# Even attention: the keys' low part written once, and the heads' norms with joined diagonals, joined epsilons and a root of eight operations

## Chip, cores and metric

The kernel runs on one core of one Trainium2 chip. The metric is the device time of one execution in microseconds (us), lower is better. The time given for a kernel is the median of its runs. One execution was also recorded by the hardware profiler, and all rows of the profile are of that one. Engines carry the profile's names: PE is TensorE's matmuls and PEld its weight loads, DVE is VectorE, ACT is ScalarE, POOL is GpSimd, SP is SyncE (here it issues DMAs).

## What is computed

The reference is a small transformer of two layers in float32: 512 tokens (`x`) and 256 context tokens (`ctx`) of width 1024, each layer with a mixer and a gated feed-forward network, every part with a modulated norm in front. The change touches the mixer of layer 0, the even one. Beside a gated chunk network it holds a differential attention with four heads: each head has two components of 64 channels, two softmaxes over the 768 keys, and takes their difference.

```python
def diff_attn(q, k, v, lam):
    b, tq = q.shape[0], q.shape[1]
    tk = k.shape[1]
    s = jnp.einsum('bqhd,bkhd->bhqk', q, k).astype(jnp.float32) * ATTN_SCALE
    p = jax.nn.softmax(s, axis=-1).reshape(b, B_HEADS, 2, tq, tk)
    a = p[:, :, 0] - lam * p[:, :, 1]
    return jnp.einsum('bhqk,bkhe->bqhe', a.astype(v.dtype), v)

def diff_out(o, g, lam_init):
    b, t = o.shape[0], o.shape[1]
    return (rmsnorm(o, g) * (1.0 - lam_init)).reshape(b, t, B_V_WIDTH)
```

The 512 token queries see all 768 keys, the 256 context queries only the 256 context keys. `rmsnorm` divides by the root of the mean square plus 1e-6.

## The kernel before

**Layout.** Activations lie with channels on the 128 partitions and tokens along the free axis, 768 of them (512 tokens, then 256 context). A head's two components of 64 channels share one tile: component 0 on partitions 0 to 63, component 1 on 64 to 127.

**Products in two parts.** To keep float32 accuracy with the faster `float32r` matmuls, an operand is split into a rounded high part (a cast on ACT) and the remainder (a subtraction on DVE or POOL). A full product is three matmuls (`mm3`, L110 to 116): high by high, high by low, low by high.

**Scores.** For scores the split uses the spare rows of the 64-channel contraction. `stack_q` (L267) makes one 128-row tile per component: the query's high part on that component's own 64 partitions, its low part on the other 64. `stack_k` (L280) makes two tiles per component: `kh` with the key's high part on both halves, `kl` with the key's low part on both halves. Two accumulating passes over 128 rows, Q by `kh` and Q by `kl`, then give all four products. `kh` takes two ACT casts of 64x768 (L286, L287), `kl` two DVE subtractions of 64x768 (L289). All four key tiles of a head come from one tag of six buffers, the query tiles from a tag of three.

**A head.** `head` (L621) runs three query pairs. `attend` (L566) calls `softmax_diff` (L541) for two blocks of 128 queries: per component the two passes (L550 to 553; 512 token keys by L552, only for the first four blocks, and 256 context keys by L553), the row maximum on DVE (L554), the exponential on ACT with its row sum (L556), then on DVE the difference of the components (L560 to 562) and an epsilon for the later norm (L563: the square of the first component's sum times 1e-6, since the probabilities are left undivided). PE transposes the result (L574), ACT and DVE split it (L130, L131), and PE multiplies it with the split values (L114 to 116); ACT copies the head's output out (L586).

**Norm of a head.** It follows one head later, in steps: squares on ACT (L611), then `rstd_diag` (L153): matmuls with a tile of ones sum the squares over channels (L164), DVE adds the epsilons (L175), takes the inverse root by three Newton steps from an integer estimate (`rsqrt_small`, L139 to 148, ten instructions), and writes six 128x128 diagonals, one per block of tokens (L184); two matmuls of ones by the diagonals spread the factors over all partitions (L194), and DVE applies them (L619).

**Order of the work.** The code gives each instruction a priority, in the order in which it is written, but for blocks that are raised or held back explicitly. A planner then simulates the engines with durations of its own and gives each engine's queue, step by step, the instruction that can run, the more urgent first; a tile can be written as soon as a buffer of its tag is free. On the chip each queue runs strictly in the order found. Within `head`, the stacking of the next head is written behind the second query pair. To fill PE beside the attention there are the projections of the gated network (`gated`, L588; its weights are cast by ACT at L88 and L91's subtraction is done by POOL), gelu on ACT (L642), and transposes with statistics on DVE (`turn`, L648). All of this runs roughly from 150 to 330 us of the span. The odd attention of layer 1 (L1584 to L1633) is not touched.

Of the kernel before, what the change touches and what calls it, by code (L numbers as in the profile page):

```python
# [6 lines left out]
F32 = mybir.dt.float32  # L7
F32R = mybir.dt.float32r
BF16 = mybir.dt.bfloat16
I32 = mybir.dt.int32  # L10
AF = mybir.ActivationFunctionType
ALU = mybir.AluOpType
AX = mybir.AxisListType.X

P = 128
D = 1024
KT = D // P
TX = 512
TC = 256
TA = TX + TC  # L20
HID = 2816
NF = HID // P
EPS = 1e-6
ROOT = 0.703952253
# [3 lines left out]
class Builder:  # L28
# [251 lines left out]
    def stack_k(self, k, pool, T, tag, bufs):  # L280
        nc = self.nc
        out = []
        for X, Y in ((slice(0, 64), slice(64, 128)), (slice(64, 128), slice(0, 64))):
            kh = pool.tile([P, T], F32R, name=self.uid("kh"), tag=tag, bufs=bufs)
            kl = pool.tile([P, T], F32R, name=self.uid("kl"), tag=tag, bufs=bufs)
            nc.scalar.copy(kh[X], k[X])  # L286
            nc.scalar.copy(kh[Y], k[X])  # L287
            for Z in (X, Y):
                nc.vector.tensor_tensor(kl[Z], k[X], kh[X].bitcast(F32), ALU.subtract)  # L289
            out.append((kh, kl))  # L290
        return out


# [38 lines left out]
    def even(self):  # L332
        tc, nc, a = self.tc, self.nc, self.a
# [7 lines left out]
        def f3(tag="f3", bufs=8):  # L341
            return R1.tile([P, TA], F32, name=self.uid(tag), tag=tag, bufs=bufs)
# [4 lines left out]
        for k in range(0, KT, 2):  # L347
            t = self.load(Rh, a["xT"][k * P:(k + 2) * P, :].rearrange("(k p) t -> p k t", p=P), [P, 2, TX], f"hx{k}")
# [47 lines left out]
        sq = self.squares(hx, TX)  # L396
# [24 lines left out]
        qk = {}  # L421
# [37 lines left out]
        for half, heads in enumerate(((0, 1), (2, 3))):  # L459
# [3 lines left out]
            for k in range(KT):  # L463
                t = self.adap.tile([P, 2, 512], F32R, name=self.uid("wq"), tag="wq", bufs=3) if k % 3 == 2 else None
# [8 lines left out]
                if half == 0:  # L473
                    t, sh = hx[k], self.modcol(0, 0, k, 0)
# [35 lines left out]
        for k in range(KT):  # L510
            W = self.unit(a["v0"][k * P:(k + 1) * P, :], 512)
            for tb in range(6):
                c = slice(tb * P, (tb + 1) * P)
# [24 lines left out]
        Ra = tc.alloc_tile_pool(name="att0", bufs=1, side="right", reuse_waits="tile")  # L538
        oraw, raw = [], {}

        def softmax_diff(Q, K, qb, eps):  # L541


            koff = 0 if qb < 4 else TX
            qs = slice(qb * P, (qb + 1) * P)
            nm, sums = self.small(2, "sa", 10), self.small(2, "sa", 10)
            es = []
            for c in range(2):
                ps = self.wide()
                for p in range(2):  # L550
                    if qb < 4:
                        nc.tensor.matmul(ps[:, :TX], Q[c][:, qs], K[c][p][:, :TX], start=p == 0, stop=p == 1)  # L552
                    nc.tensor.matmul(ps[:, TX:TA], Q[c][:, qs], K[c][p][:, TX:], start=p == 0, stop=p == 1)  # L553
                nc.vector.tensor_reduce(nm[:, c:c + 1], ps[:, koff:TA], axis=AX, op=ALU.max, negate=True)  # L554
                e = Ra.tile([P, TA], F32, name=self.uid("e"), tag="e", bufs=6)
                self.last_exp = nc.scalar.activation(e[:, koff:], ps[:, koff:TA], AF.Exp, bias=nm[:, c:c + 1],  # L556
                                                     accum_out=sums[:, c:c + 1])
                es.append(e[:, koff:])
            r = self.small(1, "sa", 10)
            nc.vector.reciprocal(r, sums[:, 1:2])  # L560
            nc.vector.scalar_tensor_tensor(r, r, self.nlam, sums[:, 0:1], ALU.mult, ALU.mult)
            nc.vector.scalar_tensor_tensor(es[0], es[1], r, es[0], ALU.mult, ALU.add)
            nc.vector.scalar_tensor_tensor(eps[:, qb:qb + 1], sums[:, 0:1], EPS, sums[:, 0:1], ALU.mult, ALU.mult)  # L563
            return es[0]

        def attend(t, Q, K, qp, o, eps):  # L566
            es = [softmax_diff(Q, K, 2 * qp + i, eps) for i in range(2)]
            kbs = list(range(6)) if qp < 2 else [4, 5]
            po = self.bank()[:, :TC]
            for i in range(0, len(kbs), 2):  # L570
                pt = self.bank()
                for j in range(2):
                    for b in range(2):
                        nc.tensor.transpose(pt[:, j * TC + b * P:j * TC + (b + 1) * P],  # L574
                                            es[b][:, (i + j) * P:(i + j + 1) * P], self.ident)
                th = Ra.tile([P, 512], F32R, name=self.uid("ath"), tag="at", bufs=6)
                tl = Ra.tile([P, 512], F32R, name=self.uid("atl"), tag="at", bufs=6)
                self.split(th, tl, pt)
                for j in range(2):
                    kb = kbs[i + j]  # L580
                    c = slice(t * P, (t + 1) * P)
                    m = slice(j * TC, (j + 1) * TC)
                    self.mm3(po, (vhi[kb][:, c], vlo[kb][:, c]), (th[:, m], tl[:, m]),
                             i + j == 0, i + j == len(kbs) - 1)
            s = slice(qp * TC, (qp + 1) * TC)
            nc.scalar.copy(o[:, s], po)  # L586
# [10 lines left out]

        def stack(t):
            return (self.stack_q(qk[t], Ra, TA, "sq", 3, eng=nc.gpsimd if t == 3 else nc.vector),
                    self.stack_k(qk[4 + t], Ra, TA, "sk", 6))  # L600

        norms = {}

        def norm(t, step):

            if t not in norms:
                return
            o, eps = norms[t][:2]
            if step == 0:
                sq = self.sumsq()  # L610
                nc.scalar.activation(sq, o, AF.Square)  # L611
                norms[t] = o, eps, sq
            elif step == 1:
                sq = norms[t][2]
                norms[t] = o, eps, self.rstd_diag([(sq[:, :TX], TX), (sq[:, TX:], TC)], 1.0 / P, eps=eps)
            else:
                for off, T, dg in ((0, TX, norms[t][2][0]), (TX, TC, norms[t][2][1])):
                    c = o[:, off:off + T]
                    nc.vector.scalar_tensor_tensor(c, c, self.subg, self.spread(dg), ALU.mult, ALU.mult)  # L619

        def head(t):  # L621
            Q, K = QK.pop(t)
            o = f3("o", 4)
            eps = self.small(6, "sx", 2)
            for qp in range(3):
                attend(t, Q, K, qp, o, eps)
                if qp == 0:
                    norm(t - 1, 1)
                elif qp == 1:
                    if t < 3:  # L630
                        QK[t + 1] = stack(t + 1)
                    norm(t - 1, 2)
            norms[t] = o, eps
            norm(t, 0)
            if t == 3:
                norm(t, 1)
                norm(t, 2)
            oraw.append(o)
# [38 lines left out]
        with tc.high_priority(offset=tc.cur_priority - here):  # L677
            QK = {0: stack(0)}
        for t in range(2):
            head(t)  # L680
# [5 lines left out]
        with tc.high_priority(offset=tc.cur_priority - here), tc.issue_after(last.ins):  # L686
            head(2)
            head(3)
# [48 lines left out]
        sq, rest = self.sumsq(), []  # L737
# [1072 lines left out]
```

## Time and profile before

| | |
|---|---|
| median of 3 runs | 1576.95 us (1575.58 to 1578.64) |
| profiled execution | 1580.41 us |
| its span, first to last instruction | 1578.6 us |
| mean granted clock of TensorE | 0.990 |
| instructions | 24990 |
| DMA | 162.27 MB, mean 103 GB/s |

The profile's page gives busy times as shares of the span; a busy PE is not PE at its peak, since matmuls are pipelined and their shown durations overlap. Therefore the distance from one start to the next is the measure of what a matmul costs in a full queue. Rows of the timeline give the start, the duration, the engine, the line, the operation, output and inputs, and behind them in brackets the idle time of the engine just before and the instruction that ended it. Rows of a line's view give the count and the shortest, median and longest duration in ns. `L49` stands for lines of helpers that many parts share.

### The profile page before, as it was taken

The numbers are of one execution on the slowest core, as the hardware profiler recorded it, in microseconds if no ns is written. First come the engines' busy times: TensorE is split into PE (matmuls) and PEld (weight loads), VectorE is DVE, ScalarE is ACT, GpSimd is POOL, SyncE is SP. The second block draws the span as 40 slices with busy tenths as digits, with TensorE's granted clock in tenths as the row PEclk, the third lists the DMA queues.
The fourth block names the chain that finished last, engine by engine and source line by source line (L and its number), as shares of the span: only waits on it lengthen the run. The fifth ranks groups of instructions, "written<-read, shape, count | busy, mean of one in ns | idle before, by whom it ended". The sixth has DMA issues, their size and how long they took to land.

```text
span 1578.6 us, 24990 instructions
## 1 busy us (share of the span) xinstructions
PE 1517.3 (96%) x9563; PEld 1356.5 (86%) x9563; DVE 1078.7 (68%) x1938; ACT 727.8 (46%) x1490; POOL 826.8 (52%) x558
## 2 busy tenths in 40 slices
PE   6999988999999999999999999899999999999998
PEld 4776877889989999999999988677869889999997
DVE  4620788775697787888886486765667876666665
ACT  2422677553552333333333354555645644444444
POOL 0464211050347767767776544531314299898882
PEclk9999998999999999999999999999999999999999
DMA  8735100043123333345542211200225133333201
GB/s 330 310 129 202 44 8 1 1 134 134 67 74 114 113 102 127 127 146 168 162 158 88 79 47 36 66 28 15 68 87 207 48 105 105 105 99 109 93 21 54
DMA packets 53416, 162.27 MB, mean 103 GB/s; under 512 B 6192, under 2 KB 8624, under 8 KB 45616
## 3 DMA queue, kind: packets, MB, share of 16 engines
q1 hardware_dynamic: 46240, 135.37, 25.6%
q10 hardware_dynamic: 7056, 25.30, 4.9%
q8 instruction: 75, 1.23, 0.3%
q14 instruction: 45, 0.37, 0.1%
HBM read 158.55 MB, written 2.10 MB: 102 GB/s over the span
## 4 chain that ended last, share of the span: by engine, by line
PE 85%; DVE 10%; ACT 3%; issue 1%; DMA 0%; POOL 0%; DVEq 0%; SPq 0%; ACTq 0%; POOLq 0%
PE pw L114 12%; PE pw L115 12%; PE pw L116 11%; PE pb L115 8%; PE pb L116 8%; PE pb L114 8%; PE pf L114 4%; PE pf L115 4%; PE pf L116 4%; PE pb L1633 2%; PE pb L1622 2%; PE pf L369 2%; PE pw L1584 1%; PE pw L1592 1%; DVE t L49 1%
## 5 line engine op out<-in xcount | busy, mean ns | idle before, releaser
L115 PE MATMUL pw<-ax,w 128*128 128x384 f32 (+2 forms) x740 | 236.6, 320 | 4.2 <-DVE ax L49 2.2
L114 PE MATMUL pw<-ax,w 128*128 128x384 f32 (+2 forms) x740 | 235.8, 322 | 3.6 <-DVE q L49 1.9
L116 PE MATMUL pw<-ax,w 128*128 128x384 f32 (+2 forms) x740 | 236.1, 320 | 0.1
L784 DVE SCALAR_TENSOR_TENSOR xT<-pb,mod,xT 128x512 f32<-128x512 f32 (+3 forms) x204 | 143.2, 708 | 127.7 <-PE pb L116 127.3
L91 POOL TENSOR_TENSOR w<-raw,w 128x512 fp32r<-128x512 f32 (+1 forms) x76 | 114.9, 1521 | 218.2 <-ACT w L88 195.6
L49 POOL TENSOR_TENSOR w<-raw,w 128x512 fp32r<-128x512 f32 x122 | 185.9, 1539 | 48.5 <-ACT w L49 48.3
L49 POOL TENSOR_TENSOR w<-t,w 128x512 fp32r<-128x512 f32 x99 | 148.7, 1505 | 55.6 <-ACT w L49 55.6
L114 PE MATMUL pb<-hh,w 128*128 128x512 f32 x480 | 170.9, 356 | 2.3 <-DVE xT L784 2.3
L116 PE MATMUL pb<-hh,w 128*128 128x512 f32 x480 | 171.4, 357 | 0.0
L115 PE MATMUL pb<-hh,w 128*128 128x512 f32 x480 | 171.1, 356 | 0.0
L115 PE MATMUL pw<-T,w 128*128 128x384 f32 (+1 forms) x508 | 158.3, 312 | 2.3 <-DVE T L131 2.3
L114 PE MATMUL pw<-T,w 128*128 128x384 f32 (+1 forms) x508 | 157.8, 312 | 2.0 <-ACT T L130 1.5
L116 PE MATMUL pw<-T,w 128*128 128x384 f32 (+1 forms) x508 | 158.2, 312 | 0.0
L115 PEld LDWEIGHTS pw<-ax,w 128*128 128x128 f32 x740 | 140.7, 190 | 10.6 <-DVE ax L49 2.7
L114 PEld LDWEIGHTS pw<-ax,w 128*128 128x128 f32 x740 | 139.8, 190 | 10.8 <-DVE q L49 2.7
L114 PE MATMUL pf<-ax,w 128*128 128x256 f32 (+2 forms) x428 | 141.5, 331 | 4.2 <-ACT f L595 2.8
L116 PEld LDWEIGHTS pw<-ax,w 128*128 128x128 f32 x740 | 140.4, 190 | 3.5 <-DVE w L953 0.4
L115 PE MATMUL pf<-ax,w 128*128 128x256 f32 (+2 forms) x428 | 140.3, 328 | 0.0
L116 PE MATMUL pf<-ax,w 128*128 128x256 f32 (+2 forms) x428 | 140.1, 327 | 0.0
L49 POOL TENSOR_TENSOR hh<-hs,hh 128x768 fp32r<-128x768 f32 (+1 forms) x42 | 78.3, 1866 | 95.0 <-ACT hh L49 93.5
L49 POOL TENSOR_TENSOR w<-rawo,w 128x512 fp32r<-128x512 f32 x59 | 103.6, 1757 | 29.8 <-ACT w L49 29.8
L239 DVE SCALAR_TENSOR_TENSOR junk<-ar,cb 128x1024 bf16<-128x1024 f32 x64 | 105.7, 1651 | 0.0
(410 smaller groups left out, 3920.5 us busy)
## 6 DMA issues: line engine op xcount, KB each, us to landing
raw<-ffn_in SPq DMA_DIRECT2D x44, 1024.0 KB, 5.4
ar<-ada SPq DMA_DIRECT2D x24, 1024.0 KB, 7.4
ar<-ada ACTq DMA_DIRECT2D x48, 512.0 KB, 3.6
rawo<-ffn_out SPq DMA_DIRECT2D x88, 256.0 KB, 3.0
raw<-odd_out SPq DMA_DIRECT2D x32, 256.0 KB, 2.7
raw<-qk SPq DMA_DIRECT2D x16, 256.0 KB, 7.8
raw<-uv SPq DMA_DIRECT2D x16, 256.0 KB, 2.8
raw<-even_out SPq DMA_DIRECT2D x8, 512.0 KB, 3.9
```

Source lines behind the costliest of these rows:

```text
L49: self.tail[key] = fn(*args, **kw)
L91: eng.tensor_tensor(lo, raw, hi.bitcast(F32), ALU.subtract)
L114: mm(out, s[0], m[0], start=start, stop=False, **kw)
L115: mm(out, s[0], m[1], start=False, stop=False, **kw)
L116: return mm(out, s[1], m[0], start=False, stop=stop, **kw)
L239: return self.nc.vector.scalar_tensor_tensor(junk, t, 1.0, self.cb[who], ALU.mult, ALU.mult, accum_out=self.acc[who][:, col:col + 1])
L369: nc.tensor.matmul(ps[32 * q:32 * q + 32, :w], cst[:, k, :], t[:, w * q:w * q + w], start=k == 0, stop=k == KT - 1, skip_group_check=True)
L784: ins = self.nc.vector.scalar_tensor_tensor(h, ps[:, r], self.modcol(l, j, m, who), h, ALU.mult, ALU.add)
L1584: nc.tensor.matmul(ps[:, st:en], Q, K[g][p][:, b0 * P:b1 * P], start=p == 0, stop=p == 1, skip_group_check=True)
L1592: last = nc.tensor.matmul(ps[:, en:en + TC], Q, K[g][p][:, TX:], start=p == 0 and not edge, stop=p == 1, skip_group_check=True)
L1622: last = nc.tensor.transpose(pt[:, x * P:(x + 1) * P], es[2 * (x % 2) + x // 2][:, kb * P:(kb + 1) * P], self.ident)
L1633: nc.tensor.matmul(po[64 * h:64 * h + 64, :], V[vb][:, 64 * g:64 * g + 64], t[:, h * TC:h * TC + TC], start=kb == 0, stop=kb == nb - 1, sk ...
```

## The change

In `stack_k` the low part of the keys is written once: one tile `low` per head, component 0's remainder on partitions 0 to 63 and component 1's on 64 to 127, by two subtractions instead of four. Each pass now comes with the rows that it uses: the pass over `kh` uses all 128, the pass over `low` only the component's own 64, so that the product of the two low parts is left out. The tags become four buffers for `kh` and two for `low`.

In `softmax_diff` the row sums go straight into one tile per head (12 columns), and the epsilon instruction per block is gone. `head_diag` takes the place of `rstd_diag` for the heads: it makes all six epsilons in one instruction, takes the inverse root in eight instructions with other constants, and writes the diagonals in two instructions (four blocks and two) that multiply the identity, repeated, by the factors, repeated.

```diff
     def stack_k(self, k, pool, T, tag, bufs):
         nc = self.nc
         out = []
+        low = pool.tile([P, T], F32R, name=self.uid("kl"), tag="kl", bufs=2)
         for X, Y in ((slice(0, 64), slice(64, 128)), (slice(64, 128), slice(0, 64))):
             kh = pool.tile([P, T], F32R, name=self.uid("kh"), tag=tag, bufs=bufs)
-            kl = pool.tile([P, T], F32R, name=self.uid("kl"), tag=tag, bufs=bufs)
             nc.scalar.copy(kh[X], k[X])
             nc.scalar.copy(kh[Y], k[X])
-            for Z in (X, Y):
-                nc.vector.tensor_tensor(kl[Z], k[X], kh[X].bitcast(F32), ALU.subtract)
-            out.append((kh, kl))
+            nc.vector.tensor_tensor(low[X], k[X], kh[X].bitcast(F32), ALU.subtract)
+            out.append(((slice(0, P), kh), (X, low)))
         return out
...
-        def softmax_diff(Q, K, qb, eps):
+        def softmax_diff(Q, K, qb, sums):
...
-            nm, sums = self.small(2, "sa", 10), self.small(2, "sa", 10)
+            nm, sums = self.small(2, "sa", 10), sums[:, 2 * qb:2 * qb + 2]
...
-                for p in range(2):
+                for p, (r, k) in enumerate(K[c]):
                     if qb < 4:
-                        nc.tensor.matmul(ps[:, :TX], Q[c][:, qs], K[c][p][:, :TX], start=p == 0, stop=p == 1)
-                    nc.tensor.matmul(ps[:, TX:TA], Q[c][:, qs], K[c][p][:, TX:], start=p == 0, stop=p == 1)
+                        nc.tensor.matmul(ps[:, :TX], Q[c][r, qs], k[r, :TX], start=p == 0, stop=p == 1)
+                    nc.tensor.matmul(ps[:, TX:TA], Q[c][r, qs], k[r, TX:], start=p == 0, stop=p == 1)
...
-            nc.vector.scalar_tensor_tensor(eps[:, qb:qb + 1], sums[:, 0:1], EPS, sums[:, 0:1], ALU.mult, ALU.mult)
...
-                    self.stack_k(qk[4 + t], Ra, TA, "sk", 6))
+                    self.stack_k(qk[4 + t], Ra, TA, "kh", 4))
...
+        def head_diag(sq, sums):
+
+            ve = nc.vector
+            v, y, u = self.small(6), self.small(6), self.small(6)
+            s0 = sums[:, :12].rearrange("p (n c) -> p n c", c=2)[:, :, 0]
+            ve.scalar_tensor_tensor(u, s0, EPS, s0, ALU.mult, ALU.mult)
+            for o, n in ((0, 4), (4, 2)):
+                ps = self.bank()
+                for j in range(n):
+                    c = slice(j * P, (j + 1) * P)
+                    self.last_sum = nc.tensor.matmul(ps[:, c], sq[:, (o + j) * P:(o + j + 1) * P], self.ones, start=j == 0,
+                                                     stop=True, skip_group_check=True)
+                col = ps[:, :n * P].rearrange("p (j f) -> p j f", f=P)[:, :, 0]
+                ve.scalar_tensor_tensor(v[:, o:o + n], col, 1.0 / P, u[:, o:o + n], ALU.mult, ALU.add)
+            ve.tensor_scalar(y.bitcast(I32), v.bitcast(I32), -0.5, float(0x5F1FFFF9), ALU.mult, ALU.add)
+            ve.tensor_tensor(u, y, y, ALU.mult)
+            ve.scalar_tensor_tensor(u, u, -1.0, v, ALU.mult, ALU.mult)
+            ve.scalar_tensor_tensor(y, u, 2.38924456, y, ALU.add, ALU.mult)
+            ve.tensor_tensor(u, y, y, ALU.mult)
+            ve.scalar_tensor_tensor(u, u, ROOT * ROOT, v, ALU.mult, ALU.mult)
+            ve.scalar_tensor_tensor(u, u, -10.0 / 3.0, u, ALU.add, ALU.mult)
+            ve.scalar_tensor_tensor(y, u, 5.0, y, ALU.add, ALU.mult)
+            dgs = []
+            for o, n in ((0, 4), (4, 2)):
+                dg = self.tmp()[:, :n * P]
+                self.last_diag = ve.scalar_tensor_tensor(
+                    dg.rearrange("p (j f) -> p j f", f=P), y[:, o:o + n].unsqueeze(2).to_broadcast([P, n, P]), 0.375 * ROOT,
+                    self.ident.unsqueeze(1).to_broadcast([P, n, P]), ALU.mult, ALU.mult)
+                dgs.append(dg)
+            return dgs
...
-                norms[t] = o, eps, self.rstd_diag([(sq[:, :TX], TX), (sq[:, TX:], TC)], 1.0 / P, eps=eps)
+                norms[t] = o, eps, head_diag(sq, eps)
...
-            eps = self.small(6, "sx", 2)
+            eps = self.small(12, "sx", 2)
```

## The prediction

> **What bounds the kernel now.** I read the page first: busy shares and the chain that ended last.
>
> ```profile
> PE 1517.3 (96%) x9563; PEld 1356.5 (86%) x9563; DVE 1078.7 (68%) x1938; ACT 727.8 (46%) x1490; POOL 826.8 (52%) x558
> PE 85%; DVE 10%; ACT 3%; issue 1%; DMA 0%; POOL 0%; DVEq 0%; SPq 0%; ACTq 0%; POOLq 0%
> ```
>
> TensorE (PE) is busy nearly throughout and carries 85% of the chain, so over the whole kernel an edit counts by what it adds to or takes from PE's time. But these are averages. The change lies in the even attention, so I next took the view of windows there, with one window of the later, steady part for contrast. Its columns are the length, then busy time and instruction count of PE, PEld, DVE, ACT, POOL, then the granted clock, the DMA share and GB/s.
>
> ```profile
> 160.00:200.00 40.00, 39.02 (x228) 33.55 (x226) 30.14 (x54) 25.39 (x49) 9.92 (x6) 1.00 0.14 40
> 200.00:240.00 40.00, 33.31 (x212) 29.30 (x212) 33.53 (x74) 29.66 (x60) 6.79 (x4) 0.96 0.03 8
> 240.00:280.00 40.00, 33.91 (x181) 28.68 (x182) 33.74 (x94) 26.31 (x54) 6.48 (x4) 0.87 0.00 1
> 280.00:320.00 40.00, 38.84 (x255) 33.78 (x254) 29.40 (x97) 23.15 (x48) 0.00 (x0) 1.00 0.02 4
> 520.00:560.00 40.00, 40.00 (x229) 37.96 (x229) 30.37 (x41) 13.99 (x27) 29.68 (x18) 1.00 0.39 122
> ```
>
> From 520 us PE never idles; from 200 to 280 us it idles 12.8 of 80 us (40 - 33.31 and 40 - 33.91), and its clock falls to 0.87. This is the stage in which VectorE (DVE) and ScalarE (ACT) matter. Narrower windows find the holes:
>
> ```profile
> 195.00:205.00 10.00, 6.68 (x42) 5.36 (x42) 9.17 (x19) 9.37 (x19) 0.00 (x0) 1.00 0.01 2
> 225.00:235.00 10.00, 6.60 (x44) 5.44 (x44) 8.87 (x26) 7.81 (x18) 1.29 (x1) 0.94 0.00 0
> 235.00:245.00 10.00, 6.14 (x30) 4.72 (x29) 9.11 (x22) 9.89 (x15) 1.89 (x1) 0.84 0.00 0
> 270.00:275.00 5.00, 2.38 (x15) 1.88 (x14) 4.96 (x12) 3.77 (x10) 2.03 (x1) 0.97 0.00 0
> 150.00:330.00 180.00, 163.60 (x973) 140.08 (x973) 138.20 (x355) 117.31 (x232) 25.89 (x17) 0.96 0.09 29
> ```
>
> PE's idle time in the four holes is 3.3 + 3.4 + 3.9 + 2.6 = 13.2 us, most of the 16.4 us (180 - 163.6) of the whole stage. In the holes DVE is busy nine tenths and ACT up to 99%. Three of them are the places where one head ends and the next begins; the third (235 to 245) is filled by ACT's gelu:
>
> ```profile
> 236.33 3.05 ACT L642 ACTIVATE f<-f 128x768 f32<-128x768 f32 x4
> ```
>
> The timeline of the second hole shows why; a bracket names the idle time before the row and who ended it.
>
> ```profile
> 228.87 0.83 ACT L286 CAST kh<-f 64x768 fp32r<-64x768 f32 x1 [0.47 <-PE pw L553]
> 229.72 0.83 ACT L287 CAST kh<-f 64x768 fp32r<-64x768 f32 x1
> 230.58 0.84 ACT L272 ACTIVATE qb<-f 64x768 fp32r<-64x768 f32 x1
> 231.44 0.47 ACT L556 ACTIVATE e<-pw,sa 128x256 f32<-128x256 f32 x1
> 229.73 1.92 DVE L289 TENSOR_TENSOR kl<-f,kh 64x768 fp32r<-64x768 f32 x2
> 232.06 0.39 PE L553 MATMUL pw<-kh,qb 128*128 128x256 f32 x1 [2.54 <-ACT e L556]
> ```
>
> The second half of the next head's keys can be cast only when a score matmul of the old head (L553) has released the key buffer; three casts in a row (2.5 us) then stand in ACT's queue ahead of the exponential L556 that PE needs. The last hole is built the same way, and in the first PE waits behind such casts too:
>
> ```profile
> 268.51 0.83 ACT L286 CAST kh<-f 64x768 fp32r<-64x768 f32 x1 [0.42 <-PE pw L553]
> 271.48 0.47 ACT L556 ACTIVATE e<-pw,sa 128x256 f32<-128x256 f32 x1
> 272.19 0.47 PE L552 MATMUL pw<-kh,qa 128*128 128x512 f32 x1 [1.66 <-ACT e L556]
> ```
>
> ```profile
> 201.03 0.49 PE L552 MATMUL pw<-kh,qa 128*128 128x512 f32 x1 [1.37 <-ACT e L556]
> ```
>
> **The change part by part.**
>
> *DVE instructions.* The rows with the old and new forms:
>
> ```profile
> L289 DVE TENSOR_TENSOR kl<-f,kh x16: 942/954/1773, 158.5 to 270.6; 64x768 fp32r<-64x768 f32 x16
> L563 DVE SCALAR_TENSOR_TENSOR sx<-sa x24: 146/158/1250, 172.5 to 303.0; 128x1 f32<-128x1 f32 x24
> L184 DVE TENSOR_SCALAR q<-ident,sm x40: 278/283/1839, 16.2 to 1220.8; 128x128 f32<-128x128 f32 x40
> L49 DVE SCALAR_TENSOR_TENSOR q<-sm,ident 128x512 f32<-128x512 f32 x1 | 0.7, 694 | 0.0
> L49 DVE SCALAR_TENSOR_TENSOR q<-sm,ident 128x256 f32<-128x256 f32 x1 | 0.4, 425 | 0.0
> L145 DVE TENSOR_TENSOR sm<-sm 128x6 f32<-128x6 f32 x12 | 1.9, 162 | 0.2
> ```
>
> Per head, by medians: two of four key remainders go, 2 x 0.954 = 1.91 us. Six epsilon instructions become one (strided, 128x6, priced like L145): 6 x 0.158 - 0.16 = 0.79 us. Six diagonals of 0.283 us become two joined ones, whose form the kernel has once elsewhere at 0.694 and 0.425 us: 1.70 - 1.12 = 0.58 us. The root goes from ten to eight instructions of about 0.162 us: 0.32 us. Together 3.6 us per head and 14.4 us of DVE work in four heads. Most of it lies beside PE work: DVE is busy 138.2 of the stage's 180 us, PE 163.6. Only what is in a hole counts, and there ACT comes first. I take 1 us for epsilons, diagonals and root together, with bounds 0 and 3 (the four holes take 35 of the stage's 180 us, a fifth, and a fifth of 14.4 us is 2.9).
>
> *Buffers.* Six key buffers of one tag, four used per head, become four for the high and two for the low part, two and one used per head. So both halves of the next head's keys can be made while the present head runs, and only its second query tile (three buffers, unchanged) still waits for the old head's last matmuls. In the second and last hole two casts (L286, L287: 1.66 us) leave the row of three ahead of the exponential, and in the first PE's 1.37 us behind the casts can go: 1.66 + 1.66 + 1.37 = 4.7 us. Where DVE was next, one remainder of 0.95 us instead of two follows the query's. I take 6 us for the heads' ends. ACT's cast count does not fall (four per head), so the casts only move to other times, at worst into another hole: the lower bound is 0. The upper is 9: two thirds of the idle 13.2 us, since gelu and the query cast stay. PE's low clock in the holes (0.84 between 235 and 245 us) would gain with it; that is inside these bounds' width, and I count nothing for it.
>
> *The second score pass on 64 rows.* Before, both passes use all 128 rows. After, the first does, and the second uses rows 0 to 63 or 64 to 127 alone. The counts:
>
> ```profile
> L553 PE MATMUL pw<-kl,qa x24: 277/280/415, 170.1 to 300.4; 128*128 128x256 f32 x24
> ```
>
> There are as many with `qb`, so 48 excursions from 128x128 to a half array and back. The columns streamed stay the same, so no time is saved by halving the rows, and two half passes do not stand side by side in the code, since the first pass of the other component lies between them: below nothing is excluded. No row of before shows a 64-row pass. The nearest rows are those of the odd attention, which goes to 64 *columns* and back:
>
> ```profile
> 1088.63 0.65 PE L1633 MATMUL pb<-pt,v 128*64 128x256 f32 x4
> 1089.22 0.44 PE L1584 MATMUL pw<-kh,qb 128*128 128x384 f32 x1
> ...
> 1090.01 0.28 PE L1592 MATMUL pw<-kl,qb 128*128 128x256 f32 x1
> 1090.22 1.08 PE L1633 MATMUL pb<-pt,v 128*64 128x256 f32 x8
> 1091.23 0.39 PE L1584 MATMUL pw<-kh,qa 128*128 128x256 f32 x1
> 1091.45 0.28 PE L1584 MATMUL pw<-kl,qa 128*128 128x256 f32 x1
> ```
>
> ```profile
> 266.83 0.28 PE L114 MATMUL pb<-ath,vhi 128*128 128x256 f32 x1
> 266.95 0.28 PE L115 MATMUL pb<-atl,vhi 128*128 128x256 f32 x1
> ```
>
> Starts are the measure, as matmuls overlap. In steady 128x128 work a 256-column matmul starts 0.12 us after the last. Going in takes 1090.22 - 1090.01 = 0.21, so 0.09 more. Eight narrow ones hold PE 1.01 us and four hold it 0.59; four more cost 0.42, so leaving costs 0.59 - 0.42 = 0.17. The first matmul afterwards takes 0.22 to the next start, 0.10 more. One excursion: 0.09 + 0.17 + 0.10 = 0.36 us; 48 of them: 17.3 us. Bounds: 0 (a half of the rows is not such a change) and 17.3. I take the upper, as the only rows of any partial array in this trace show the cost each time. Not all of it is felt: where PE would otherwise idle, it is free. PE was busy 163.6 of 180 us at a clock of 0.96, so some nine tenths at the most; score passes stand next to the waits more often than other matmuls, and I take seven tenths: 12 us. If the holes close, this cover is gone and it is up to nine tenths, 15.6 us.
>
> [...]
>
> *Sum.* 12 - 6 - 1 = +5 us on the profiled execution, which took 1580.41 us (span 1578.6, 1.8 us around it) and lies 3.5 us above the median, 1576.95. As a difference it carries over: 1576.95 + 5 = **1582.0 us**. What is late next in the stage is PE itself, which no longer has idle time to give.
>
> **The rivals.**
>
> *Half rows are free (ends faster).* [...] Then only the gains stand: 6 + 1 = 7 us, between 0 and 12 by the bounds: 1570 us. It decides at a price of 7 / (0.7 x 48) = 0.21 us per excursion: below that the change gains. For it: rows and columns of the array need not behave alike. Against: every excursion to a partial array in this trace pays.
>
> *Costs and gains cancel.* The switch costs half of the column one, or hides in waits to a half (8 us), against 7 us: 1578 us. For it: DVE and ACT have slack as soon as PE is the slower.
>
> *The holes stay.* ACT's casts move, but stand in front of other exponentials; the query tile still waits. For it: the cast count and the three query buffers are unchanged, and ACT is the busier engine in the third hole. Then 15.6 - 1 = about +14, or 1591 us at the most, 1588 at the middle.
>
> That the change does not do what it says I leave at next to nothing: by the code 16 remainders become 8 and the heads' 24 diagonals become 8. A further scatter comes from the planner, which may order the stage's fill matmuls anew; it is inside the ranges.
>
> **How the numbers follow.** Forecast 0.40 (1579 to 1586 by itself); half rows free 0.31; cancel 0.17; holes stay 0.12. About 0.2% (3.2 us) is what a measurement of this kernel can tell from no change, so faster is below 1573.8 and slower above 1580.1. Faster: nearly all of the second case and a little of the third, 0.33. Same: most of the third and an edge of the forecast, 0.17. Slower: 0.50. The range leaves out the ends: 1567 (gains of 10 at no cost) to 1591.
>
> **What would show it.** Right, if the starts around a 64-row matmul stand about 0.1 us further apart going in and 0.2 to 0.3 coming out, PE's busy time of the stage grows by about 10 us or more, and the holes at the heads' ends shrink with no cast waiting for L553. Wrong, if the start of the matmul behind a half pass keeps to 0.12 us after 256 columns (then the free rival), or if key casts still stand in a row ahead of an exponential (then the holes stay). DVE's busy time should fall by about 14 us in any case. If it does not, my prices for DVE are wrong.

## The result: 17.5 us slower

The changed kernel takes 1594.57 us (median of four runs, 1592.39 to 1596.23), the kernel before 1577.11 us (1575.58 to 1578.64). The ratio is 1.0106, 95% interval 1.0092 to 1.0120. The forecast of 1582 had the sign right; the range ended at 1591. The profiled execution took 1594.86 us, with a span of 1593.1 us.

The page of the kernel after, busy times and the chain that ended last:

```profile
PE 1537.5 (97%) x9563; PEld 1358.8 (85%) x9563; DVE 1064.0 (67%) x1886; ACT 727.3 (46%) x1490; POOL 825.0 (52%) x558
PE 86%; DVE 9%; ACT 3%; issue 2%; DMA 0%; POOL 0%; DVEq 0%; SPq 0%; ACTq 0%; POOLq 0%
```

As many matmuls as before (9563), but PE is busy 20.2 us longer. DVE lost 52 instructions and 14.7 us, close to the 14.4 of the forecast, and the time went up all the same. The windows that the prediction showed, of the kernel after:

```profile
200.00:240.00 40.00, 37.46 (x213) 28.99 (x211) 28.29 (x60) 27.77 (x58) 5.27 (x4) 0.97 0.03 8
240.00:280.00 40.00, 35.24 (x183) 26.84 (x182) 27.92 (x68) 26.92 (x55) 6.54 (x4) 0.88 0.00 1
280.00:320.00 40.00, 39.33 (x195) 30.09 (x194) 25.82 (x74) 15.74 (x36) 0.00 (x0) 0.89 0.00 1
520.00:560.00 40.00, 40.00 (x233) 38.32 (x232) 31.92 (x46) 13.94 (x26) 27.62 (x17) 1.00 0.35 110
```

In the window from 520 us PE is full at full clock, as before. In the attention DVE has more room, but PE does fewer matmuls in a window: 195 instead of 255 from 280 to 320 us, at a clock of 0.89 instead of 1.00. To compare like with like I take the stage by its work, from the first score matmul to the first matmul of the gated network's mixing, one window for each kernel (columns as in the prediction: length, then busy time and instruction count of PE, PEld, DVE, ACT, POOL, then clock, DMA share, GB/s). Before:

```profile
169.50:331.70 162.20, 145.81 (x889) 126.06 (x889) 125.95 (x338) 104.89 (x215) 22.18 (x14) 0.96 0.08 26
```

After:

```profile
169.60:346.90 177.30, 165.27 (x890) 128.44 (x889) 115.54 (x289) 102.90 (x213) 20.28 (x15) 0.94 0.07 25
```

The stage is 15.1 us longer (177.3 - 162.2), and of the profiled executions' difference (1594.86 - 1580.41 = 14.5 us) nothing is left to look for elsewhere. Inside it PE works 19.5 us longer on the same matmuls, and its idle time falls from 16.4 to 12.0 us. So PE's matmuls became dearer. The timeline of one score group on PE, first before, then after:

```profile
181.09 0.28 PE L553 MATMUL pw<-kh,qa 128*128 128x256 f32 x1
181.21 0.39 PE L552 MATMUL pw<-kl,qa 128*128 128x512 f32 x1
181.44 0.28 PE L553 MATMUL pw<-kl,qa 128*128 128x256 f32 x1
181.55 0.39 PE L552 MATMUL pw<-kh,qb 128*128 128x512 f32 x1
181.78 0.28 PE L553 MATMUL pw<-kh,qb 128*128 128x256 f32 x1
```

```profile
182.74 0.28 PE L552 MATMUL pw<-kh,qa 128*128 128x256 f32 x1
182.95 0.50 PE L551 MATMUL pw<-kl,qa 64*128 64x512 f32 x1
183.29 0.27 PE L552 MATMUL pw<-kl,qa 64*128 64x256 f32 x1
183.49 0.50 PE L551 MATMUL pw<-kh,qb 128*128 128x512 f32 x1
183.82 0.28 PE L552 MATMUL pw<-kh,qb 128*128 128x256 f32 x1
```

Read the starts. Into the half pass 0.21 us instead of 0.12, its first matmul 0.34 instead of 0.23, out of it 0.20 instead of 0.11 to 0.12, the first full matmul 0.33 instead of 0.23: 0.09 + 0.11 + 0.08 + 0.10 = 0.38 us for one excursion to 64 rows. Most of the others come to 0.34 to 0.40 us by the same reading. The trace holds 49 of them (48 by the code; in one, other work stands between the two half matmuls), together 18.6 us at this price. PEld shows what is gone. Before, the weights of a pass are loaded ahead of it (these from 181.09 us, for the matmul at 181.21; for the 80 matmuls over the low part 0.03 to 0.43 us ahead); after, the first matmul of each of the 49 excursions starts within 0.002 us of the start of its weight load. First before, then after:

```profile
181.09 0.19 PEld L552 LDWEIGHTS pw<-kl,qa 128*128 128x128 f32 x1
```

```profile
182.95 0.18 PEld L551 LDWEIGHTS pw<-kl,qa 64*128 64x128 f32 x1 [0.25 <-issue]
```

The expected gain did appear at the heads' ends, where now only the query cast waits for the old head's last score matmul:

```profile
235.48 0.84 ACT L272 ACTIVATE qb<-f 64x768 fp32r<-64x768 f32 x1 [0.25 <-PE pw L552]
276.07 0.84 ACT L272 ACTIVATE qb<-f 64x768 fp32r<-64x768 f32 x1 [0.57 <-PE pw L552]
```

The freed key casts, however, went into another hole. ACT has them in a row behind gelu, ahead of the cast of `ath` that PE needs (ACT, and PE's row at the end):

```profile
242.11 0.83 ACT L271 ACTIVATE qa<-f 64x768 fp32r<-64x768 f32 x1
242.85 0.82 ACT L286 CAST kh<-f 64x768 fp32r<-64x768 f32 x1
...
245.38 0.83 ACT L287 CAST kh<-f 64x768 fp32r<-64x768 f32 x1
246.12 0.57 ACT L130 CAST ath<-pb 128x512 fp32r<-128x512 f32 x1
246.74 0.39 PE L114 MATMUL pb<-ath,vhi 128*128 128x256 f32 x1 [2.62 <-ACT ath L130]
```

**Theory**: the switch of the array between 128 and 64 rows costs all of the 17.5 us, and the rest of the change gains nothing because the casts only moved. **Rivals**: the norms or the new buffers cost something too; or the 64-row matmuls are slow by themselves, not the switches; or the gain exists and the switch costs even more.

### The profile page after: what moved, and what is told of

Same layout as the page of the kernel before. It is cut to its first block, busy times and chain, and to the rows that moved or that the text cites. A ratio compares the mean times of both kernels' runs of the same rounds, so it can differ in the third digit from the quotient of the medians.

```text
span 1593.1 us, 24944 instructions
## 1 busy us (share of the span) xinstructions
PE 1537.5 (97%) x9563; PEld 1358.8 (85%) x9563; DVE 1064.0 (67%) x1886; ACT 727.3 (46%) x1490; POOL 825.0 (52%) x558
## 4 chain that ended last, share of the span: by engine, by line
PE 86%; DVE 9%; ACT 3%; issue 2%; DMA 0%; POOL 0%; DVEq 0%; SPq 0%; ACTq 0%; POOLq 0%
PE pw L114 11%; PE pw L115 11%; PE pw L116 11%; PE pb L115 8%; PE pb L114 8%; PE pb L116 8%; PE pf L114 4%; PE pf L115 4%; PE pf L116 4%; PE pb L1662 2%; PE pb L1651 2%; PE pf L368 2%; PE pw L551 1%; PE pw L1613 1%; PE pw L1621 1%
```

## The experiments

In the diffs, lines that begin with - are those of the kernel named.

**1. The change with full rows.** The kernel after, but the second pass uses all 128 rows.

```diff
-            out.append(((slice(0, P), kh), (X, low)))
+            out.append(((slice(0, P), kh), (slice(0, P), low)))
```

> The changed kernel, but the second score pass reads all 128 rows of the shared low tile; the rows of the other component add products of two low parts, which is another small term in place of the one left out. No 64-row pass is left, all else is as in the change. Theory (the 48 excursions to a 64-row array cost 0.38 us each, nearly all of it felt, and the rest of the change gains a little): 3 to 5 us below the kernel before, about 1573. Rival (the excursions are hidden to a third and cost 12, and the rest of the change, casts moved into the gelu hole and a new order, costs 5): about 1582.

1577.39 us (1574.41 to 1580.22); against before (1577.61) 0.9997, interval 0.9986 to 1.0009. One edit takes the whole slowdown away, 1594.57 - 1577.39 = 17.2 us, and what remains of the change shows no gain. The time lies between the theory's 1573 and the rival's 1582. Its stage:

```profile
168.30:329.50 161.20, 144.38 (x890) 124.60 (x889) 114.69 (x289) 102.40 (x213) 20.84 (x15) 0.97 0.08 27
```

DVE has 11.3 us less to do than before (125.95 - 114.69) and PE idles as long: 16.8 us, 16.4 before. Where the gain went, the gelu shows. It starts on ACT, in the kernel before and then in this one:

```profile
235.03 1.28 ACT L642 ACT_TABLE_LOAD   x1
```

```profile
229.59 1.28 ACT L671 ACT_TABLE_LOAD   x1
...
234.56 0.81 ACT L286 CAST kh<-f 64x768 fp32r<-64x768 f32 x1
...
237.09 0.83 ACT L287 CAST kh<-f 64x768 fp32r<-64x768 f32 x1
237.83 0.58 ACT L130 CAST ath<-pb 128x512 fp32r<-128x512 f32 x1
238.46 0.58 PE L114 MATMUL pb<-ath,vhi 128*128 128x256 f32 x1 [4.99 <-ACT ath L130]
```

By the gelu, two heads' ends are behind, PE has done nearly the same work (372 matmuls from the stage's start, 370 here), and the kernel is 5.4 us ahead (235.03 - 229.59), 1.2 us of which it had at the stage's start (169.5 - 168.3). So 4.2 us were gained, of 6 us forecast for all of them. Then a table load, gelu and five casts stand in a row on ACT (the rows above leave out the gelu and three of the casts), and PE waits 4.99 us in one piece for what is behind them. The window around it:

```profile
230.00:240.00 10.00, 4.00 (x24) 3.11 (x23) 8.71 (x21) 9.91 (x13) 1.80 (x1) 0.88 0.00 0
```

6.0 us idle, where the window of the gelu before (235 to 245 us) had 3.9. At the stage's end 1.0 us is left of the gain (162.2 - 161.2).

**2. Half rows alone.** The kernel before, with its buffers, remainders and norms; only the second pass uses the component's own 64 rows, so that the product of the low parts is left out as in the change.

```diff
-            out.append((kh, kl))
+            out.append(((slice(0, P), kh), (X, kl)))
...
-                for p in range(2):
+                for p, (r, k) in enumerate(K[c]):
...
-                    nc.tensor.matmul(ps[:, TX:TA], Q[c][:, qs], K[c][p][:, TX:], start=p == 0, stop=p == 1)
+                    nc.tensor.matmul(ps[:, TX:TA], Q[c][r, qs], k[r, TX:], start=p == 0, stop=p == 1)
```

> The kernel before with one edit: the second score pass uses only the component's own 64 rows of queries and low keys. Writes, buffers and norms are as before. Theory: 48 x 0.38 = 18 us slower, 1592 to 1598. Rival (a third hidden): 12 us slower, about 1589.

1591.50 us (1586.99 to 1594.40); 1.0087, interval 1.0068 to 1.0106: 13.9 us slower. The switch alone does it. It costs less than in the changed kernel, and the stage has less idle time left:

```profile
170.20:342.00 171.80, 162.41 (x888) 127.24 (x888) 127.38 (x338) 105.05 (x214) 21.03 (x14) 0.95 0.07 25
```

171.80 - 162.41 = 9.4 us idle instead of 16.4: about 7 us of the switches (49 in this trace too, 18.6 us) lie where PE would have waited. The stage of this one profiled execution is 9.6 us longer, less than the medians' 13.9; the executions of this kernel spread over 7 us.

**3. and 4. The other two parts alone.** Experiment 3 is the kernel after with the old `stack_k` and the old full passes, so that only the norms are new. Experiment 4 is the kernel before with the low part written once and the new buffers (passes on full rows), so that only the norms are old. Of each edit one line is shown.

```diff
-                    self.stack_k(qk[4 + t], Ra, TA, "kh", 4))
+                    self.stack_k(qk[4 + t], Ra, TA, "sk", 6))
```

> Only the norm part of the change: joined epsilons, joined diagonals, root of eight operations, row sums in one tile per head; keys and passes as before. Theory: DVE has 6.8 us less work (4 x 1.69), little of it in a hole: within 2 us of before, rather faster. Rival (the new order of the planner costs): 2 to 5 us slower.

```diff
-                    self.stack_k(qk[4 + t], Ra, TA, "sk", 6))
+                    self.stack_k(qk[4 + t], Ra, TA, "kh", 4))
```

> Only the key part of the change, but with the second pass over all 128 rows of the shared low tile (the same small extra term): low part written once, four buffers for the high and two for the low part, norms as before. Theory: the holes at two heads' ends shrink: 2 to 4 us faster than before. Rival (the casts that move into the gelu hole cost as much as they save, or more): 0 to 5 us slower.

Norms alone: 1579.16 us (1576.24 to 1581.77), 1.0008, interval 0.9999 to 1.0018. Keys alone: 1579.27 us (1575.90 to 1582.86), 1.0012, interval 1.0002 to 1.0022. Neither gains, so the 2 to 4 us expected of the keys did not come; both lie a little above experiment 1, which holds both. The stages of their profiled executions are 161.5 and 161.2 us long, experiment 1's is 161.2, so differences of 2 us do not show in the stage; I leave them unexplained.

**5. Fewer switches.** The kernel after, with the passes of component 1 in the other order, so that the two half passes of a block, on different rows, follow each other.

```diff
-                for p, (r, k) in enumerate(K[c]):
+                for p, (r, k) in enumerate(K[c][::-1] if c else K[c]):
```

> The changed kernel with the second component's passes in the other order: full and half for component 0, half and full for component 1. The two half passes stand next to each other, so 24 excursions to a 64-row array instead of 48, with the same matmuls. Theory (a fixed price of 0.38 us per excursion, nearly all felt): 24 x 0.38 = 9 us below the changed kernel, about 1585; if the two half passes, on different rows, also run side by side, up to 6 us less, about 1580. Rival (a 64-row matmul is slow in itself): no change, about 1594.

1587.33 us (1584.76 to 1589.20); 1.0059, interval 1.0045 to 1.0073, so 7.2 us below the kernel after. The planner put other matmuls between many of the pairs, and the trace has 38 excursions instead of 49: 11 x 0.38 = 4.2 us. Where pairs stayed together, two half passes on different rows start at the same instant:

```profile
181.38 0.50 PE L551 MATMUL pw<-kl,qa 64*128 64x512 f32 x1
181.38 0.49 PE L551 MATMUL pw<-kl,qb 64*128 64x512 f32 x1
181.72 0.27 PE L552 MATMUL pw<-kl,qa 64*128 64x256 f32 x1
181.72 0.28 PE L552 MATMUL pw<-kl,qb 64*128 64x256 f32 x1
```

Of such pairs of matmuls the trace has 16 (two of them start 0.05 us apart). Each saves a start distance of 0.12 or 0.23 us (256 or 512 columns), together some 2.6 us. That 4.2 + 2.6 comes near to 7.2 may be chance, though. The profiled execution (1584.76 us, the fastest of the four) has this stage:

```profile
169.40:338.60 169.20, 154.40 (x889) 122.91 (x888) 114.22 (x289) 102.86 (x213) 20.16 (x14) 0.97 0.07 26
```

It is 8.1 us shorter than the stage of the kernel after (177.3 - 169.2), its clock is 0.97 instead of 0.94, and its idle time 14.8 us instead of 12.0. A good part of the gain is thus the clock; experiment 6 shows how much.

**6. More switches.** The kernel after, with the passes alternating for every part of the keys. The matmuls are the same, as many on 64 rows; only their order gives 80 excursions, by the code and in the trace.

```diff
-                for p, (r, k) in enumerate(K[c]):
-                    if qb < 4:
-                        nc.tensor.matmul(ps[:, :TX], Q[c][r, qs], k[r, :TX], start=p == 0, stop=p == 1)
-                    nc.tensor.matmul(ps[:, TX:TA], Q[c][r, qs], k[r, TX:], start=p == 0, stop=p == 1)
+                for s in ((slice(0, TX), slice(TX, TA)) if qb < 4 else (slice(TX, TA),)):
+                    for p, (r, k) in enumerate(K[c]):
+                        nc.tensor.matmul(ps[:, s], Q[c][r, qs], k[r, s], start=p == 0, stop=p == 1)
```

> The changed kernel with the order of the four matmuls of a component changed for the 16 blocks with token keys: full and half over the 512 token keys, then full and half over the 256 context keys. Same matmuls, 32 more excursions (80 instead of 48). Theory: 32 x 0.38 = 12 us above the changed kernel, about 1607. Rival (a 64-row matmul is slow in itself, or the cost is hidden): within 3 us of it.

1609.47 us (1608.28 to 1610.58); 1.0200, interval 1.0187 to 1.0214: 14.9 us above the kernel after for 32 more excursions, 0.47 each. That settles it: not the 64-row matmul is slow, but each change of the row count. The 0.47 is not the price of the change alone, as the clock falls with it (below).

```profile
182.47 0.40 PE L551 MATMUL pw<-kh,qa 128*128 128x512 f32 x1
182.80 0.50 PE L551 MATMUL pw<-kl,qa 64*128 64x512 f32 x1
183.23 0.38 PE L551 MATMUL pw<-kh,qa 128*128 128x256 f32 x1
183.54 0.38 PE L551 MATMUL pw<-kl,qa 64*128 64x256 f32 x1
183.85 0.50 PE L551 MATMUL pw<-kh,qb 128*128 128x512 f32 x1
```

From the third on, every row starts 0.2 us later than the columns of the row before it need (0.43 for 512, 0.31 for 256, against 0.23 and 0.12). With 0, 48 and 80 excursions the kernels take 1577.4, 1594.6 and 1609.5 us. The stage shows that more than the switches grows:

```profile
168.00:362.60 194.60, 184.38 (x889) 136.04 (x888) 116.58 (x289) 103.14 (x212) 19.66 (x14) 0.90 0.07 22
```

The clock of 0.90 is a mean over the stage. In these traces the granted clock is either 1.00 or 0.50, and narrow windows find the stretches at 0.50. After, there are three in the stage:

```profile
237.86:244.69 6.83, 6.26 (x24) 4.70 (x22) 5.62 (x13) 6.78 (x9) 1.62 (x1) 0.50 0.00 0
248.10:251.50 3.40, 3.40 (x9) 2.03 (x9) 1.94 (x11) 2.72 (x6) 0.00 (x0) 0.50 0.00 0
278.82:289.06 10.24, 9.98 (x31) 7.10 (x29) 7.22 (x26) 3.96 (x11) 0.03 (x1) 0.50 0.01 2
```

In experiment 1 there are two:

```profile
237.55:244.37 6.82, 5.76 (x16) 4.15 (x17) 4.80 (x15) 5.27 (x10) 0.00 (x0) 0.50 0.00 0
268.27:271.68 3.41, 2.85 (x9) 2.49 (x10) 3.31 (x14) 1.37 (x5) 0.00 (x0) 0.50 0.03 5
```

In this kernel there are four (from 229.89, 243.55, 257.20 and 291.33 us). Half of such time counts as lost; what remains of the stage is PE's time at full clock.

| excursions by the code | stage | PE idle in it | at half clock | lost by it | the rest |
|---|---|---|---|---|---|
| 0 (experiment 1) | 161.2 us | 16.8 us | 10.2 us | 5.1 us | 139.3 us |
| 48 (after) | 177.3 us | 12.0 us | 20.5 us | 10.2 us | 155.1 us |
| 80 (experiment 6) | 194.6 us | 10.2 us | 37.6 us | 18.8 us | 165.6 us |

PE's time at full clock grows by 15.8 and 26.3 us, about 0.33 us per excursion and so a little less than the starts gave. The switches do fill idle time, 4.8 and 6.6 us of it, but the loss to the halved clock grows by 5.1 and 13.7 us. The table is of the profiled executions, and good to about 1 us, since in some of the halved time PE idles. Experiment 5's stage has 10.2 us at half clock, as experiment 1 has: of the 8.1 us by which it is shorter than the stage after, 5.1 are the clock.

**7. and 8. Casts later.** If the gelu hole took the gain, holding the casts back should bring it. Both kernels are experiment 1 with the stacking of the next head ordered behind the last exponential written so far: 7 for head 3's alone (`t == 2`), 8 for every head's. Experiment 8's edit:

```diff
-                        QK[t + 1] = stack(t + 1)
+                        with tc.issue_after(self.last_exp.ins):
+                            QK[t + 1] = stack(t + 1)
```

> The kernel with full rows on the shared low tile (e1), with one order more: the casts for the last head's queries and keys are queued on ACT behind the exponentials of head 2's second pair, not behind the gelu. Theory (e1 gained 5 us by head 1's end and lost 3 of them when five casts in a row stood behind the gelu and PE waited 5 us): the hole shrinks by 2 to 4 us, 1573 to 1576. Rival (what e1 lost in heads 2 and 3 has other causes): within 1 us of e1, 1577.

> As the run before, for all heads: each next head's casts are queued behind the exponentials of the present head's second pair. Theory: the six casts in a row at head 0's end go too; 2 to 6 us below e1, 1571 to 1575. Rival (the casts fill idle time of ACT where they are, and later they delay the next head): slower than e1 by 1 to 5 us.

1574.18 us (1572.67 to 1578.47), 0.9984, interval 0.9973 to 0.9994; and 1574.22 us (1573.72 to 1576.52), 0.9980, interval 0.9971 to 0.9989. Stage and PE of experiment 8:

```profile
170.00:327.80 157.80, 143.75 (x890) 125.91 (x889) 118.66 (x291) 106.48 (x218) 20.24 (x13) 0.97 0.08 26
```

Idle time is 14.0 us instead of 16.8, and the stage is 3.4 us shorter than in experiment 1. Both beat the kernel before, by 2.5 and 3.2 us by their ratios, and are the fastest versions found. Against experiment 1 they gain 3 us, which is at the edge: the intervals to the kernel before overlap a little. Holding back every head's casts gains no more than holding back head 3's alone. In experiment 7 PE's longest wait by the gelu is 2.40 us, where experiment 1 had 4.99. Of the 7 us forecast about half was to be had in this way.

**9. and 10. The same order on the other kernels.** Is it the order that gains, or the order with the new buffers? Experiment 9 has experiment 8's edit in the kernel before, experiment 10 has it in experiment 4 (new keys, old norms).

> The kernel before with the order of the casts alone: each next head's casts are queued on ACT behind the exponentials of the present head's second pair. Theory (the gain of that order needs the buffers of the change; with the old six buffers the second half of the casts waits for the old head's last matmuls in any case): within 2 us of before, 1576 to 1580. Rival (the order alone makes the gain): about 1574.

> The key part with full rows and the later casts, norms as before; against the same with the change's norms (1574.2). Theory (VectorE does not bound the stage, so 6.8 us less norm work on it buys nothing): the same within 1.5 us, 1573 to 1576. Rival (the norms' shorter work counts once the casts are out of the way): 2 to 4 us slower, 1576 to 1578.

Experiment 9 takes 1585.27 us (1583.17 to 1586.38), 1.0057, interval 1.0044 to 1.0070. That is neither the theory's number nor the rival's: I had expected no change or a gain, and it is 8.5 us slower. With six buffers of one tag, key casts and a query cast still stand in a row of three at the second head's end, as the timeline of ACT shows:

```profile
231.62 0.83 ACT L286 CAST kh<-f 64x768 fp32r<-64x768 f32 x1
232.47 0.83 ACT L287 CAST kh<-f 64x768 fp32r<-64x768 f32 x1
233.33 0.84 ACT L272 ACTIVATE qb<-f 64x768 fp32r<-64x768 f32 x1
```

That row does not explain the loss: the kernel before has the same one (228.87 to 231.42 us, in the prediction), and PE's wait beside it is shorter here, 1.73 us against 2.54. The profiled execution is only 2.8 us above that of before (1583.17 - 1580.41). Why this order costs the old kernel 8.5 us stays open.

Experiment 10 takes 1575.35 us, 0.9990, interval 0.9974 to 1.0006; its runs scatter more, from 1568.98 to 1580.83. Between 9 and 10 lie 9.9 us, and they differ in the keys' part alone: that part of the change is of use, but only with another order than the one it came with. Whether that is its buffers or its two remainders fewer was not tried apart. Between 10 and 8 lie the new norms, and their 1.1 us can't be told from nothing.

## Why the prediction was wrong in size

**Right: the switch and its price.** Rows of the array pay as columns do: 0.36 us was carried over from the 128x64 matmuls, 0.38 was found. The prediction's 0.17 for leaving shows as two parts, 0.11 at the first half matmul and 0.08 on the way out; its 0.09 going in and 0.10 at the first full matmul were found as they were. Of the cause the trace shows this much: the first half matmul starts within 0.002 us of its weight load, where before the weights were loaded 0.03 to 0.43 us ahead. The other reading, that half rows cost nothing, fell: going in alone takes 0.09 us and the first half matmul 0.11 us more than in full rows, and with that fell the rival of free half rows. DVE's 14.4 us were right (14.7), and so was that key casts would no longer wait at the heads' ends.

**Wrong, first: "I take 6 us for the heads' ends" and 1 us for the norms.** Together they measured 0 (experiment 1 lies 0.2 us below before, well inside its interval). The prediction had the reason in hand as its lower bound: casts move, "at worst into another hole". That is what happened. The heads' ends had given 4.2 us by the gelu, and the gelu's own hole, which the prediction had seen and set aside as unchanged, took most of it back. The third rival, "the holes stay", was nearer than the forecast. The norms alone (experiment 3) show no gain.

**Wrong, second: "I take seven tenths: 12 us", in which the clock has no part.** The edit cost 17.2 us (after minus experiment 1). The table has the stage's 16.1 us of it: +15.8 us of PE's time at full clock, -4.8 us of idle time filled, +5.1 us lost to the halved clock. The first two make 11.0 us, near the 12 of the forecast; since the share of seven tenths was a guess, that is in part luck. What was missing is the third term.

**Wrong, third: the clock.** The prediction saw the low clock in the holes (0.84 between 235 and 245 us), counted it as a possible gain only, and put it at nothing. It went the other way, 0.96 to 0.94 in the stage. This is also why the high end was too low: 15.6 - 1 had nearly all cover gone, but neither a clock that costs nor gains of nothing.

The sum again, with what was measured: +17.2 for the switch (its clock included), 0 for the heads' ends and the norms, against 17.5 us measured. The forecast was 12 - 6 - 1.

Open: why the clock stays low for longer with half passes. The table shows that it does, and no run changed the clock alone. That time goes with the clock shows in one kernel too: experiment 10's executions of 1568.98 to 1570.91 us had a mean clock of 0.995 or 0.996, those of 1580.43 to 1580.83 us one of 0.988. The four of the kernel after do not line up like that (1594.27 us at 0.988, 1596.23 at 0.991). Open too is why experiments 3 and 4 do not lie at experiment 1's time, and why experiment 9 is slower than before.

## What to carry to other kernels

Price a change of the array's shape by the starts around it, count it for every switch and not for every matmul, and do not count on idle time nearby: it hid a part here (4.8 us after, 6.6 in experiment 6), but the loss to the halved clock grew by as much or more (5.1 and 13.7 us). In a stream of 128-row matmuls, a pass that needs only 64 rows was cheaper on all 128 with a small extra term (by 17.2 us for the 48 half passes); failing that, half passes on different rows belong next to each other (7.2 us below the kernel after in experiment 5). When an edit sets work free to start earlier, ask into which queue and ahead of whom it goes next; here the new keys gained only when the casts were also held back.

## What the runs showed of the hardware

Two 64-row matmuls on different halves of the array start within 0.01 us of each other and run side by side (experiment 5, 14 of the 16 pairs): two of 512 columns start at 181.38 us and the next two at 181.72, 0.34 us for both, where in the kernel after one alone takes 0.34 (182.95 to 183.29). The switch to 64 rows and back, 0.38 us, takes more than such pairs save (at most 0.35 us, 0.12 + 0.23).

In the kernel after the clock stays low over a stretch in which PE has almost no idle time. From 280 to 290 us, before and then after:

```profile
280.00:290.00 10.00, 10.00 (x63) 8.73 (x62) 7.33 (x16) 3.69 (x8) 0.00 (x0) 1.00 0.00 0
```

```profile
280.00:290.00 10.00, 10.00 (x31) 7.30 (x31) 6.98 (x23) 2.78 (x6) 0.00 (x0) 0.55 0.01 2
```

Half the matmuls in the same 10 us, PE shown busy for all of them, at a mean clock of 0.55. Nine of the 10 us lie in the stretch of 10.24 us at 0.50, in which PE is busy for 9.98 us; it begins 1.3 us after a wait of PE of 1.04 us has ended (at 277.5). A busy time alone does not show this; the count of instructions and the clock do.
